# First modulation quarters as columns straight from the matrix engine, in a one-core hybrid encoder block

## The chip, the cores and the metric

The kernel runs on one core of a Trainium2 chip. The metric is the device time of one execution in microseconds (us). Engines are called PE (matrix engine), PEld (its weight loads), DVE (VectorE), ACT (ScalarE), POOL (GpSimd) and SP (the queue that issues most DMAs).

## The reference

One encoder layer on x of 1024 tokens by 1024 channels: a SwiGLU feed-forward, an attention mixer with two branches, and a second SwiGLU. Each of the three is modulated by shift, scale and gate vectors that come from one conditioning vector c. Only the start matters here:

```python
cond = jax.nn.silu(c)
mod = (cond @ ada_w[l] + ada_b[l]).reshape(B, N_SUBLAYERS, 3, D_MODEL)
h = modulate(x, norm_g[l, 0], mod[:, 0, 0], mod[:, 0, 1])      # rms_norm(x)*g*(1+scale)+shift
x = x + 0.5 * mod[:, 0, 2][:, None, :] * swiglu(h, ffn1_w1[l], ffn1_w3[l], ffn1_w2[l])
```

So no product of the first feed-forward can start before some channels of shift (`mod[:, 0, 0]`) and scale (`mod[:, 0, 1]`) are known: for each channel a sum of 1024 products of `cond` with a column of `ada_w`, a float32 matrix of 1024 by 9216.

## The kernel before, in words

x lies transposed in SBUF, channels on partitions: eight blocks of 128 channels, each in two halves of 512 tokens. The feed-forward's products run in "fp32 with reduced precision", split into a high and a low part (`wh`, `wl` for weights, `h` for the activations; three PE instructions for one product), with a Strassen-like scheme over pairs of column blocks (`UpPair`). They write the PSUM tiles named `y` and `b`.

A block c of h is made from x by DVE (`x <- x*A*rb`, with A the scale times the norm's gain and rb the norm's inverse root spread over partitions), by ACT (`h <- x + shift`, rounded) and by DVE again (the low part). `Operands.block` does that. So block c waits for A and shift of its 128 channels, which must stand as a column, one channel on a partition.

The first 512 channels of shift and scale are made in quarters of 256 channels, by `ModQuarter`. Quarter 0 serves blocks 0 and 1, quarter 1 blocks 2 and 3. Each quarter of each vector loads four tiles `mraw` of 256 KB, each with two chunks kc of 128 rows of `ada_w` by 256 columns. Blocks 4 to 7 are served by `ModHalf` (tiles `mraw` of 128x512, sums `macc` on DVE). In the kernel before there are two ways:

- `add` (for scale): DVE multiplies each chunk by its column of `cond` and adds it into `macc` (8 instructions of 128x256). Two float32 matmuls with `ones_col` then sum over partitions and give two columns.
- `row` (for shift): PE takes a column of `cond` as the stationary operand and streams the chunk past it (8 float32 matmuls with 256 columns, one row out). ACT copies the row to `mrow`, and two small matmuls turn it into columns.

`mod_done` adds the bias `ada_b` and, for scale, forms A with a second small DVE instruction. The root of the norm (`nacc`, `nv`, `na`, `nr`, then the matmuls with `ident`) is needed beside.

The code is recorded, not issued: `Plan` collects the instructions of a phase and places them engine by engine, in an order that it works out from due times and from its own costs of each instruction (`Plan.length`). All of the first feed-forward and the modulation is one such phase. Each engine then runs its instructions strictly in the order that was placed. While `nc.inorder` is set, SP's transfers keep the order of the code: x, quarter 0, four weight tiles `wr`, quarter 1, four more `wr`, and then the tiles of the halves.

Of the kernel before, what the change touches and what calls it, by code (L numbers as in the profile page):

```python
# [17 lines left out]
AF = mybir.ActivationFunctionType  # L18
ALU = mybir.AluOpType
# [38 lines left out]
class View:  # L58


    def __init__(self, tile, ops):
        self.tile, self.ops = tile, ops
# [115 lines left out]
class Plan:  # L178
# [29 lines left out]
    def take(self, engine, op, a, kw, calls=None, took=0.0):  # L208
        if not self.on:
            return self.issue(engine, op, a, kw)  # L210
        t = Task(len(self.tasks), engine, op, a, kw)
        t.rank, t.fixed = t.i + self.behind, self.inorder and engine == "sync"
        t.calls, t.took = calls or ((op, a, kw),), took
        self.tasks.append(t)
        writes, reads = [], []
        for _, b, w in t.calls:
            writes += [v for v in (b[0], w.get("accum_out")) if isinstance(v, View)]
            reads += [v for v in list(b[1:]) + [x for n, x in w.items() if n != "accum_out"] if isinstance(v, View)]
        before = set()
        for views, write in ((reads, False), (writes, True)):  # L220
            for v in views:
                r = v.region()
                for r2, j, w2 in v.tile.log:
                    if (write or w2) and j != t.i and all(p < q2 and p2 < q for (p, q), (p2, q2) in zip(r, r2)):
                        before.add(j)
        for views, write in ((reads, False), (writes, True)):
            for v in views:
                if write and not v.ops:
                    v.tile.log = []
                v.tile.log.append((v.region(), t.i, write))  # L230
        t.ready = max([getattr(v.tile, "written", 0.0) for v in reads] + [0.0])
        tiles = {id(v.tile): v.tile for v in reads + writes + self.wanted}
        self.wanted = []
        for x in tiles.values():
            if x.t is None and x.first is None:
                t.new.append(x)
                x.first = t.i
            elif x.t is None:
                before.add(x.first)
            x.uses += 1  # L240
        t.stored = op == "dma_start" and isinstance(a[0], View) and a[0].tile.pool.space == DRAM
        t.tiles = list(tiles.values())
        t.written = [v.tile for v in writes]
        for j in before:
            self.tasks[j].after.append(t)
        t.waits = len({self.tasks[j].engine for j in before} - {engine})
        t.left = len(before)
        out = writes[0] if writes else a[0]
        shape = list(out.shape)
        t.n, t.rows = int(np.prod(shape[1:])), shape[0]  # L250
        if op == "tensor_reduce":
            t.n = int(np.prod(a[1].shape[1:]))
        t.bytes = 4 * int(np.prod(shape))
        wide = [v for v in reads if int(np.prod(v.shape[1:])) > 8]
        sb = [v for v in wide if v.tile.pool.space != PSUM]
        if engine == "gpsimd":
            t.port = bool(sb) and op != "dma_start"
        elif engine == "vector":
            if op in ("tensor_scalar", "tensor_copy", "reciprocal"):
                t.port = len(sb) == 1 and "accum_out" not in kw and writes[0].tile.pool.space != PSUM  # L260
            else:
                t.port = len(sb) >= 2
        else:
            t.port = False
        if engine == "tensor" and not took:
            m = a[2] if op == "matmul" else a[1]
            t.exact = m.tile.dt in (F32R, BF16) or any(o[0] == "bitcast" and F32R in o[1] for o in m.ops)
# [22 lines left out]
    def length(self, t, e):  # L290

        n = t.n
        if t.op == "dma_start":
            return (0.35 if e == "sync" else 0.54), 0.0
        if e == "tensor":
            if t.took:
                return t.took, 0.23
            if t.exact:
                d = max(0.04, 0.003 + n / 2286.0)
            elif t.op == "transpose":  # L300
                d = n / 1174.0
            else:
                d = max(0.224, 0.009 + n / (595.0 if t.rows > 1 else 1200.0))
            return d, 0.23
        more = "accum_out" in t.kw
        if e == "scalar":
            ap = sum(isinstance(t.kw.get(x), View) for x in ("bias", "scale"))
            start = 0.07 if isinstance(t.a[1], View) and t.a[1].tile.pool.space == PSUM else 0.11
            return start + n / 1200.0 + (0.14 if more else 0.0) + (0.06 if ap else 0.0), 0.16
        if e == "gpsimd":  # L310
            if t.op in ("tensor_scalar", "memset"):
                return 0.24 + n / 1190.0, 0.105
            return 0.06 + n / 440.0, 0.105
        if t.op == "tensor_tensor_scan":
            d = 0.15 + n / 480.0
        elif t.op == "tensor_tensor_reduce":
            d = 0.075 + n / 960.0
        elif t.op == "scalar_tensor_tensor" or more:
            d = 0.13 + n / 960.0
        elif t.op == "tensor_scalar" and t.port:  # L320
            d = 0.075 + n / 1920.0
        else:
            d = 0.07 + n / 960.0
        return max(0.2, d), 0.145
# [238 lines left out]
class SquareSum:  # L563
# [5 lines left out]
    def add(self, x):  # L569
        nc = self.k.nc  # L570
        sq = t512(self.k, name="nsq" if self.acc else "nacc")
        nc.scalar.activation(sq, x, AF.Square)
        if self.acc:
            self.eng.tensor_add(self.acc, self.acc, sq)
        else:
            self.acc = sq
        return sq
# [150 lines left out]
def t512(k, dt=F32, name="t", home="c"):  # L728

    p, tag, n = k.homes[home]  # L730
    return p.tile([128, H], dt, tag=tag, name=name, bufs=n)
# [748 lines left out]
class ModHalf:  # L1480
# [24 lines left out]
    def columns(self):  # L1505

        t = self.bank()
        for b in range(4):
            self.k.nc.tensor.matmul(t[:, b:b + 1], self.acc[:, b * 128:b * 128 + 128], self.k.ones_col, start=True, stop=True)
        mod_done(self.k, self.i, t, 4 * self.h, 4)  # L1510
# [27 lines left out]
class ModQuarter:  # L1538
# [1 line left out]

    N = 256

    def __init__(self, k, i, q, bank):
        self.k, self.i, self.q, self.bank, self.raws = k, i, q, bank, []

    def load(self, g):
        k, n = self.k, self.N
# [3 lines left out]
                            k.ada_w[g * 256:g * 256 + 256, c0:c0 + n].rearrange("(a p) n -> p a n", p=128))  # L1551
        self.raws += [t[:, 0:n], t[:, n:2 * n]]

    def add(self):
        k, nc = self.k, self.k.nc
        acc = t512(k, name="macc")[:, 0:self.N]
        for kc, t in enumerate(self.raws):
            c = k.cond[:, kc:kc + 1]
            if kc == 0:
                nc.vector.tensor_scalar(acc, t, c, None, op0=ALU.mult)  # L1560
            else:
                nc.vector.scalar_tensor_tensor(acc, t, c, acc, op0=ALU.mult, op1=ALU.add)
        self.done(acc, k.ones_col)

    def row(self):
        k, nc = self.k, self.k.nc
        t = self.bank()[0:1, 0:self.N]
        for kc, r in enumerate(self.raws):
            nc.tensor.matmul(t, k.cond[:, kc:kc + 1], r, start=kc == 0, stop=kc == 7)
        r = t512(k, name="mrow")[0:1, 0:self.N]  # L1570
        nc.scalar.activation(r, t, AF.Copy)
        self.done(r, k.ones_col[0:1, :])

    def done(self, v, one):
        t = self.bank()
        for b in range(2):
            self.k.nc.tensor.matmul(t[:, b:b + 1], v[:, b * 128:b * 128 + 128], one, start=True, stop=True)
        mod_done(self.k, self.i, t, 2 * self.q, 2)


def side_by_side(gens):
# [641 lines left out]
def layer(tc, xT, c, pos, ada_w, ada_b, ng, inv, w13a, w2a, w_a, w_f, w_q, w_g, fb, fg, dg, wbr, wout, w13b, w2b, out):  # L2223
    with ExitStack() as es:
        k = K()
# [63 lines left out]
        with ExitStack() as ph:  # L2289
# [21 lines left out]
                q.first = True  # L2311
            ops = Operands(k, 0, x, nc.vector)
            mod = {i: ModHalf(k, i, 1, bank) for i in range(2)}
            quarter = [[ModQuarter(k, i, q, bank) for i in range(2)] for q in range(2)]
            k.up_step, k.stores = 0, []

            def consts():
# [54 lines left out]
            for i in range(8):  # L2372
                t = sq.add(x[i][0])
                if i < 4:
                    nc.tensor.matmul(warm, z.bitcast(F32)[:, 0:128], x[i][0], start=True, stop=True)
            for n in range(4):
                for m in quarter[0]:
                    m.load(n)
            for i in range(2):
                pairs[i].load1("c", (0,))  # L2380
            for n in range(4):
                for m in quarter[1]:
                    m.load(n)
            for i in range(2, 4):
                pairs[i].load1("c", (0,))
            nc.inorder = False
            rms[0] = norm_rms(k, sq.acc, rp, bank)
            ops.rb[0] = norm_spread(k, rms[0], bank)
            for m in quarter:
                m[1].add()  # L2390
                m[0].row()
            for c in range(4):
                ops.block(c)
            for i in range(4):
# [323 lines left out]
```

## Time and profile before

| | us |
|---|---|
| runs | 2113.15, 2115.29, 2115.32 |
| median of these | 2115.29 |
| the profiled execution | 2112.17 |
| its span in the trace | 2110.5 |
| PE busy of the span | 2094.6 |

The span is what the trace shows of the profiled execution, 1.7 us less than its own time. [...] A row of the timeline merges equal records that follow each other and gives start, time from the first start to the last end, and their number; the bracket says how long the engine was idle before and what ended that. Where a row says mean ns, that is the length of one record, and records of PE overlap.

### The profile page before, as it was taken

The numbers are of one execution on the slowest core, as the hardware profiler recorded it, in microseconds if no ns is written. First come the engines' busy times: TensorE is split into PE (matmuls) and PEld (weight loads), VectorE is DVE, ScalarE is ACT, GpSimd is POOL, SyncE is SP. The second block draws the span as 40 slices with busy tenths as digits, with TensorE's granted clock in tenths as the row PEclk, the third lists the DMA queues.
The fourth block names the chain that finished last, engine by engine and source line by source line (L and its number), as shares of the span: only waits on it lengthen the run. The fifth ranks groups of instructions, "written<-read, shape, count | busy, mean of one in ns | idle before, by whom it ended". The sixth has DMA issues, their size and how long they took to land.

```text
span 2110.5 us, 30999 instructions
## 1 busy us (share of the span) xinstructions
PE 2094.6 (99%) x10296; PEld 1728.2 (82%) x10296; DVE 1641.7 (78%) x3167; ACT 1135.6 (54%) x2075; POOL 251.1 (12%) x397
## 2 busy tenths in 40 slices
PE   8999999999999999999999999999999999999999
PEld 5887888888888888888888888888888888888887
DVE  7989887869977399886998877979975765568554
ACT  5754444445456266688776776335543333334443
POOL 0022222321100000000444332000000000000000
PEclk9999999999999999999999999999999999999999
DMA  9468888899721555668543224794142523375511
GB/s 347 134 215 275 303 295 274 277 379 366 261 92 48 172 174 192 217 244 274 192 158 99 86 66 160 252 315 154 46 130 100 194 85 129 101 264 206 189 50 41
DMA packets 218285, 398.72 MB, mean 189 GB/s; under 512 B 27198, under 2 KB 69694, under 8 KB 217100
## 3 DMA queue, kind: packets, MB, share of 16 engines
q1 hardware_dynamic: 199772, 339.24, 48.0%
q0 software_dynamic: 18064, 57.46, 7.1%
q8 instruction: 81, 1.33, 0.3%
q14 instruction: 80, 0.66, 0.1%
q10 hardware_dynamic: 288, 0.05, 0.0%
HBM read 282.62 MB, written 114.03 MB: 188 GB/s over the span
## 4 chain that ended last, share of the span: by engine, by line
PE 91%; issue 3%; DVE 2%; DMA 2%; ACT 1%; POOL 1%; SPq 0%; POOLq 0%; DVEq 0%; ACTq 0%
PE b L198 37%; PE y L198 28%; PE pj L198 12%; PE py L198 7%; PE p L198 4%; PE pt L198 4%; DMA mraw<-in_ada_w 0%; POOL d_g L198 0%; DMA f<-d_f 0%; DMA wr<-in_w13b 0%; ACT nt L198 0%; DMA d_wf10l<-pre 0%; DVE z L198 0%; DMA x<-in_xT 0%; ACT h L198 0%
## 5 line engine op out<-in xcount | busy, mean ns | idle before, releaser
L198 PE MATMUL b<-h,wh 128*128 128x512 f32 x1408 | 436.5, 390 | 0.5 <-DVE z L198 0.4
L198 PE MATMUL y<-h,wh 128*128 128x512 f32 x1280 | 397.1, 390 | 0.4 <-ACT h L198 0.3
L198 ACT ACTIVATE wh<-wr 128x512 fp32r<-128x512 f32 x308 | 192.6, 629 | 316.0 <-PE b L198 166.1
L198 PEld LDWEIGHTS b<-h,wh 128*128 128x128 f32 x1408 | 263.2, 188 | 59.1 <-DVE z L198 3.4
L198 PEld LDWEIGHTS y<-h,wh 128*128 128x128 f32 x1280 | 239.6, 188 | 53.4 <-issue 1.2
L198 DVE TENSOR_TENSOR wl<-wr,wh 128x512 fp32r<-128x512 f32 x308 | 208.4, 686 | 94.4 <-ACT wh L198 88.8
L198 PE MATMUL b<-h,wl 128*128 128x512 f32 x704 | 273.6, 389 | 0.0
L198 PE MATMUL y<-h,wl 128*128 128x512 f32 x640 | 249.0, 389 | 0.0
L198 PE MATMUL pj<-wh,h 128*128 128x512 f32 x512 | 161.3, 391 | 0.0
L198 PEld LDWEIGHTS b<-h,wl 128*128 128x128 f32 x704 | 132.2, 188 | 27.7
L198 PEld LDWEIGHTS y<-h,wl 128*128 128x128 f32 x640 | 120.1, 188 | 24.8
L198 ACT ACTIVATE wh<-g 128x512 fp32r<-128x512 f32 x154 | 96.0, 624 | 80.2 <-PE b L198 55.7
L198 PE MATMUL b<-wh 128*128 128x512 f32 x352 | 137.0, 389 | 0.7 <-ACT mrow L198 0.7
L198 DVE TENSOR_TENSOR wl<-a,wh 128x512 fp32r<-128x512 f32 x132 | 90.8, 688 | 59.9 <-ACT wh L198 55.7
L198 PE MATMUL b<-wl,wh 128*128 128x512 f32 x352 | 136.9, 389 | 0.0
L198 PE MATMUL b<-wh,wl 128*128 128x512 f32 x352 | 136.8, 389 | 0.0
L198 ACT ACTIVATE wh<-a 128x512 fp32r<-128x512 f32 x132 | 82.4, 625 | 99.9 <-PE b L198 60.3
L198 DVE TENSOR_TENSOR wl<-g,wh 128x512 fp32r<-128x512 f32 x154 | 105.6, 686 | 29.6 <-ACT wh L198 29.1
L198 POOL TENSOR_SCALAR pr<-pr,mn 128x128 f32<-128x128 f32 (+7 forms) x128 | 102.3, 816 | 167.3 <-DVE mn L198 135.1
L198 ACT ACTIVATE pth<-pt 128x512 fp32r<-128x512 f32 (+1 forms) x160 | 85.5, 554 | 55.9 <-PE pt L198 54.3
L198 DVE TENSOR_TENSOR ptl<-pt,pth 128x512 fp32r<-128x512 f32 (+1 forms) x160 | 97.9, 632 | 20.1 <-ACT pth L198 18.6
L198 PEld LDWEIGHTS pj<-wh,h 128*128 128x128 f32 x512 | 95.7, 188 | 18.6
(382 smaller groups left out, 4376.4 us busy)
## 6 DMA issues: line engine op xcount, KB each, us to landing
g<-d_g SPq DMA_DIRECT2D x154, 256.0 KB, 5.3
mraw<-in_ada_w SPq DMA_DIRECT2D x144, 256.0 KB, 5.7
wr<-in_w13a SPq DMA_DIRECT2D x112, 256.0 KB, 5.4
wr<-in_w13b SPq DMA_DIRECT2D x88, 256.0 KB, 4.8
d_g<-z POOLq DMA_DIRECT2D x77, 256.0 KB, 5.8
d_g<-z SPq DMA_DIRECT2D x77, 256.0 KB, 3.2
a<-in_w2a SPq DMA_DIRECT2D x44, 256.0 KB, 6.3
a<-in_w2b SPq DMA_DIRECT2D x44, 256.0 KB, 5.3
```

Of the source, the lines that this page charges most:

```text
L198: getattr(getattr(self.tc.nc, engine), op)(*map(real, a), **{n: real(v) for n, v in kw.items()})
```

## The change

Both ways of making a quarter are replaced by one, `columns`: the chunk itself (128x128 of it) is the stationary operand and the column of `cond` the moving one, so that a matmul gives one column of 128 channels; eight of them add up in PSUM. That is 16 float32 matmuls with one moving column for a quarter of one vector, 64 in all. The two columns of a quarter lie in two PSUM banks, and `mod_done` is called for each of them alone. DVE's sums, the rows, ACT's copies and the small matmuls behind them are gone. The loads of a quarter come in another order: the four tiles of shift, then the four of scale, instead of taking turns.

```diff
@@ Plan.length, float32 matmuls
-                d = max(0.224, 0.009 + n / (595.0 if t.rows > 1 else 1200.0))
+                d = max(0.112, 0.005 + n / 1200.0)
@@ ModQuarter
-    def add(self):
...
-    def row(self):
...
-    def done(self, v, one):
-        t = self.bank()
+    def columns(self, *banks):
+
+        k = self.k
+        ts = [bank() for bank in banks]
         for b in range(2):
-            self.k.nc.tensor.matmul(t[:, b:b + 1], v[:, b * 128:b * 128 + 128], one, start=True, stop=True)
-        mod_done(self.k, self.i, t, 2 * self.q, 2)
+            t = ts[b % len(ts)]
+            for kc, r in enumerate(self.raws):
+                k.nc.tensor.matmul(t[:, b:b + 1], r[:, b * 128:b * 128 + 128], k.cond[:, kc:kc + 1], start=kc == 0, stop=kc == 7)
+        for b in range(len(ts)):
+            mod_done(k, self.i, ts[b][:, b:], 2 * self.q + b, 2 // len(ts))
@@ layer
-            for n in range(4):
-                for m in quarter[0]:
+            for m in quarter[0]:
+                for n in range(4):
                     m.load(n)
...
-            for m in quarter:
-                m[1].add()
-                m[0].row()
+            for q in quarter:
+                for m in q:
+                    m.columns(bank, bank)
```

The planner's cost of every float32 matmul changes too (from at least 0.224 to at least 0.112 us), so the order of the whole phase is worked out anew.

On PE, from the first `mraw` to the first products, the rows before were these (`1x256` is the row way, the `ident` row spreads the norm's root):

```order
L198 MATMUL b<-mraw,cond 1x256 x2
L198 MATMUL b<-ones_col,nacc 128x1 x4
L198 MATMUL b<-mraw,cond 1x256 x6
L198 MATMUL b<-ones_col,mrow 128x1 x2
L198 MATMUL b<-ident,nr 128x128 x4
L198 MATMUL b<-ones_col,macc 128x1 x2
L198 MATMUL b<-mraw,cond 1x256 x2
L198 MATMUL y<-h,wh 128x512 x2
```

On PE at the same place the rows now are these:

```order
L198 MATMUL b<-cond,mraw 128x1 x4
L198 MATMUL b<-ones_col,nacc 128x1 x4
L198 MATMUL b<-cond,mraw 128x1 x19
L198 MATMUL b<-ident,nr 128x128 x4
L198 MATMUL b<-cond,mraw 128x1 x9
L198 MATMUL y<-h,wh 128x512 x3
```

All 32 matmuls of quarter 0 stand ahead of the first product, 28 of them behind the norm's sum. None of quarter 1 does; before, two of its eight did.

On PE behind the first products, where quarter 1 is made between them, the rows before were these:

```order
L198 MATMUL b<-mraw,cond 1x256 x2
L198 MATMUL y<-h,wh 128x512
L198 MATMUL y<-h,wl 128x512
L198 MATMUL y<-h,wh 128x512
L198 MATMUL b<-ones_col,mrow 128x1 x2
L198 MATMUL y<-h,wl 128x512
L198 MATMUL y<-h,wh 128x512
L198 MATMUL b<-ones_col,macc 128x1 x2
```

On PE the same stretch now begins like this:

```order
L198 MATMUL y<-h,wh 128x512 x3
L198 MATMUL b<-cond,mraw 128x1 x4
L198 MATMUL y<-h,wh 128x512
L198 MATMUL y<-h,wl 128x512
L198 MATMUL b<-cond,mraw 128x1 x4
L198 MATMUL y<-h,wh 128x512
L198 MATMUL b<-cond,mraw 128x1 x4
L198 MATMUL y<-h,wh 128x512
L198 MATMUL y<-h,wl 128x512
L198 MATMUL b<-cond,mraw 128x1 x4
L198 MATMUL y<-h,wh 128x512
```

Quarter 1 now comes in eight groups of four, each between one to three products. Before it came in three groups of two behind the first product, one pair for the row and one pair for `macc`. Behind the last of the eight groups stand eleven products on blocks 0 and 1, then the first one on block 2.

On DVE the fourteen `macc<-mraw,cond,macc` of 128x256 and the two that begin them are gone. Its first `x<-x,A,b` stands behind all four small `mod` additions of quarter 0 and the A of block 0, and the first wide `macc` (128x512) stands behind the h of block 3, as it did before.

On ACT, at the end of the operands of the first feed-forward (`h<-x,mod` of its last blocks), the rows before were these:

```order
L198 ACTIVATE wh<-wr 128x512 x2
L198 ACTIVATE h<-x,mod 128x512
L198 ACTIVATE z<-y 128x512 x2
L198 ACTIVATE z<-z 128x512
L198 ACTIVATE wh<-wr 128x512
```

On ACT they now are these:

```order
L198 ACTIVATE wh<-wr 128x512
L198 ACTIVATE h<-x,mod 128x512 x2
L198 ACTIVATE z<-y 128x512
L198 ACTIVATE wh<-wr 128x512
L198 ACTIVATE z<-y 128x512
```

One more `h<-x,mod` stands ahead of the copy `z<-y` that empties a PSUM bank, and one `wh<-wr` between the two copies.

More of the change, by code (lines that the diff above doesn't have):

```diff
@@ L249, in take @@
         shape = list(out.shape)
-        t.n, t.rows = int(np.prod(shape[1:])), shape[0]
+        t.n = int(np.prod(shape[1:]))
         if op == "tensor_reduce":
@@ L1541, with __init__ @@
     N = 256
-    def __init__(self, k, i, q, bank):
-        self.k, self.i, self.q, self.bank, self.raws = k, i, q, bank, []
+    def __init__(self, k, i, q):
+        self.k, self.i, self.q, self.raws = k, i, q, []
     def load(self, g):
@@ L1552, in load @@
         self.raws += [t[:, 0:n], t[:, n:2 * n]]
-    def add(self):
[L1555 to L1563, printed above, removed]
-    def row(self):
[L1566 to L1572, printed above, removed]
-    def done(self, v, one):
-        t = self.bank()
-        for b in range(2):
-            self.k.nc.tensor.matmul(t[:, b:b + 1], v[:, b * 128:b * 128 + 128], one, start=True, stop=True)
-        mod_done(self.k, self.i, t, 2 * self.q, 2)
+    def columns(self, *banks):
+        k = self.k
+        ts = [bank() for bank in banks]
+        for b in range(2):
+            t = ts[b % len(ts)]
[3 more added lines that the diff above has]
+            mod_done(k, self.i, ts[b][:, b:], 2 * self.q + b, 2 // len(ts))
 def side_by_side(gens):
@@ L2313, in layer @@
             mod = {i: ModHalf(k, i, 1, bank) for i in range(2)}
-            quarter = [[ModQuarter(k, i, q, bank) for i in range(2)] for q in range(2)]
+            quarter = [[ModQuarter(k, i, q) for i in range(2)] for q in range(2)]
             k.up_step, k.stores = 0, []
@@ L2380, in layer @@
                 pairs[i].load1("c", (0,))
-            for n in range(4):
-                for m in quarter[1]:
+            for m in quarter[1]:
+                for n in range(4):
                     m.load(n)
```

## The prediction

> **What bounds the kernel.** First the page's busy times, then a table by stages.
>
> ```profile
> PE 2094.6 (99%) x10296; PEld 1728.2 (82%) x10296; DVE 1641.7 (78%) x3167; ACT 1135.6 (54%) x2075; POOL 251.1 (12%) x397
> ```
>
> ```profile
> 10.00:20.00 10.00, 7.35 (x42) 4.12 (x43) 9.00 (x29) 3.48 (x6) 0.00 (x0) 1.00 1.09 364
> 20.00:30.00 10.00, 9.73 (x42) 5.16 (x41) 7.75 (x18) 2.80 (x5) 0.00 (x0) 1.00 1.08 371
> 1600.00:1800.00 200.00, 200.00 (x883) 164.66 (x882) 125.46 (x197) 75.78 (x130) 0.00 (x0) 1.00 0.38 128
> ```
>
> The columns are PE, PEld, DVE, ACT and POOL busy, the granted clock, the DMA share and GB/s. PE is the bound: it has work in all but 16 us of the span of 2110.5, and from 20 us on hardly pauses, at the full clock. So a microsecond of PE work added behind the first product is a microsecond of span, and so is a delay of the first product. The change lies wholly in 10 to 35 us. There the timeline of PE is read.
>
> ```profile
> 10.95 1.02 PE L198 MATMUL b<-mraw,cond 128*1 128x256 f32 x4 [1.16 <-DMA mraw<-in_ada_w]
> 12.05 1.05 PE L198 MATMUL b<-ones_col,nacc 128*128 128x1 f32 x8
> 13.03 1.89 PE L198 MATMUL b<-mraw,cond 128*1 128x256 f32 x8
> 15.39 1.02 PE L198 MATMUL b<-mraw,cond 128*1 128x256 f32 x4 [0.47 <-DMA mraw<-in_ada_w]
> 16.88 0.60 PE L198 MATMUL b<-ones_col,mrow 1*128 1x1 f32 x4 [0.46 <-ACT mrow L198]
> 17.41 1.16 PE L198 MATMUL b<-ident,nr 128*128 128x128 f32 x8
> 18.41 0.50 PE L198 MATMUL b<-ones_col,macc 128*128 128x1 f32 x4
> 19.60 1.02 PE L198 MATMUL b<-mraw,cond 128*1 128x256 f32 x4 [0.69 <-DMA mraw<-in_ada_w]
> 20.89 0.73 PE L198 MATMUL y<-h,wh 128*128 128x512 f32 x2 [0.27 <-ACT h L198]
> ...
> 25.62 0.40 PE L198 MATMUL y<-h,wl 128*128 128x512 f32 x1
> 25.86 0.39 PE L198 MATMUL y<-h,wh 128*128 128x512 f32 x1
> 26.17 1.02 PE L198 MATMUL b<-mraw,cond 128*1 128x256 f32 x4
> 27.12 0.50 PE L198 MATMUL y<-h,wh 128*128 128x512 f32 x1
> 27.46 0.40 PE L198 MATMUL y<-h,wl 128*128 128x512 f32 x1
> 27.70 0.39 PE L198 MATMUL y<-h,wh 128*128 128x512 f32 x1
> 28.02 0.60 PE L198 MATMUL b<-ones_col,mrow 1*128 1x1 f32 x4
> 28.55 0.50 PE L198 MATMUL y<-h,wl 128*128 128x512 f32 x1
> 28.88 0.40 PE L198 MATMUL y<-h,wh 128*128 128x512 f32 x1
> 29.12 0.50 PE L198 MATMUL b<-ones_col,macc 128*128 128x1 f32 x4
> 29.48 0.49 PE L198 MATMUL y<-h,wh 128*128 128x512 f32 x1
> ```
>
> The first product comes at 20.89, released by ACT's h. From there PE takes what its queue holds, one after the other.
>
> **The price of a matmul, from grouped rows** (busy in all, then mean ns of one record):
>
> ```profile
> L198 PE MATMUL b<-mraw,cond 128*1 128x256 f32 x32 | 8.0, 378 | 2.3 <-DMA mraw<-in_ada_w 2.3
> L198 PE MATMUL b<-ones_col,mrow 1*128 1x1 f32 x8 | 1.2, 250 | 0.5 <-ACT mrow L198 0.5
> L198 PE MATMUL b<-ones_col,nacc 128*128 128x1 f32 x8 | 1.1, 253 | 0.1
> L198 DVE SCALAR_TENSOR_TENSOR macc<-mraw,cond,macc 128x256 f32<-128x256 f32 x14 | 6.7, 482 | 0.2
> L198 DVE TENSOR_SCALAR macc<-mraw,cond 128x256 f32<-128x256 f32 x2 | 0.7, 346 | 0.0
> ```
>
> The new matmul (128x128 stationary, one column moving, float32) is the form of `ones_col,nacc`: four of them are eight records, which start (1.05 - 0.25)/7 = 0.114 us apart, so 0.23 a matmul. The row way streams 256 columns past one: (1.02 - 0.38)/3 = 0.214 a record, 0.43 a matmul. The `mrow` records start (0.60 - 0.25)/3 = 0.117 apart. All of PE's share before: 32 x 0.214 + 8 x 0.117 + 8 x 0.114 (`macc`) = 8.7 us. Now: 64 x 2 x 0.114 = 14.6. So **PE gets 5.9 us more**, and DVE is rid of 6.7 + 0.7 = 7.4. The question is how much of the 5.9 falls into PE's pauses before 20.89.
>
> [...]
>
> **Term 1, the first product.** Two rows of DVE first, the last step of the norm's root and the last sums of scale:
>
> ```profile
> 16.41 0.15 DVE L198 SCALAR_TENSOR_TENSOR nr<-na,nr 128x4 f32<-128x4 f32 x1
> 16.53 1.01 DVE L198 SCALAR_TENSOR_TENSOR macc<-mraw,cond,macc 128x256 f32<-128x256 f32 x2
> ```
>
> So the root was there by 16.6 and the last tile of quarter 0 by about 17.0, when the second of these sums began. Walk the new order with these numbers. The first four matmuls start with the first tile, at 10.95 as before, and take 8 x 0.114 = 0.9. The norm's sum stays at 12.05, since it waits for DVE's `nacc`; the next work starts at 13.03. Then 19 matmuls: 38 x 0.114 = 4.3, to 17.36. The `ident` group takes 17.41 to 18.41 = 1.0, to 18.36; its input, the root, is there. Nine more matmuls: the last record starts 17 x 0.114 later, at 20.30, and ends at 20.55. PE reaches the last tile's chunks after 18.36, so it waits for no transfer. Before, the last `macc` record ended at 18.41 + 0.50 = 18.91, and this chain followed:
>
> ```profile
> 18.95 0.17 DVE mod L198
> ...
> 19.14 0.17 DVE A L198
> ...
> 19.34 0.76 DVE x L198
> ```
>
> From that end to the first product: 1.98. Now A of block 0 is done one column earlier, and x follows the fourth `mod` directly, so the step of 0.20 from `mod` to A drops out: 1.78. First product at 20.55 + 1.78 = 22.3, **1.4 later**. Bounds: if the new small operations, one column wide (the trace has two columns, 0.16 us), or the gaps come out otherwise, 0.5 to 2.0.
>
> **Term 2, quarter 1 between the products.** A group costs its records, the change of form, and slower products beside it. Around 26.17: the product before starts 0.31 ahead of the group (two products in a row: 0.23 to 0.24), the next product 0.95 behind the group's start (four records are 0.86), and that one takes 0.34 until its successor. So a group costs 0.29 besides its records. Before, behind the first product: three groups of 0.86 + 0.29, the `mrow` pair (28.55 - 27.70 less 0.23, and 0.10 behind it: 0.72) and the `macc` pair (29.48 - 28.88 less 0.23, and 0.10 again: 0.47) = 4.6. Now eight groups of 8 x 0.114 + 0.29 = 1.20: 9.6. **5.0 later.** Bounds 3.5 to 5.5, as the switch costs 0.1 or 0.3. Its DMAs land in time: PE comes to them later than before. The chain to block 2 (1.98 from its last sum) has eleven products as cover, 11 x 0.227 (200 us by 883 in the last stage quoted) = 2.5; if the cover fails, its 2.0 in part. What is lost here finds no pause of PE later in which it could be made up.
>
> **Term 3, DVE's late start.** DVE's relief is worth nothing by itself: its next wide work, the halves' sums, stands behind the h of block 3 in both orders, so it idles where `macc` was and starts these sums as late as PE comes. Then it has no slack:
>
> ```profile
> 32.80:110.90 78.10, 75.51 (x133) 1.00 0.56 190
> ```
>
> ```profile
> 109.49 0.73 ACT L198 ACTIVATE h<-x,mod 128x512 fp32r<-128x512 f32 x1 [0.40 <-DVE h L198]
> 110.88 1.26 ACT L198 ACTIVATE z<-y 128x512 f32<-128x512 f32 x2 [0.66 <-DVE h L198]
> ```
>
> ```profile
> 111.53 0.73 PE L198 MATMUL y<-h,wh 128*128 128x512 f32 x2 [0.17 <-ACT z L198]
> ```
>
> DVE is busy 75.5 of 78.1 us; ACT's `z<-y` waits for DVE, and PE for ACT's copy. The new order has one more `h<-x,mod` (0.73) ahead of this copy, and it waits for DVE too. So PE waits longer: **1.0 more**, nearest to that 0.73 with a part of DVE's step; bounds 0 (the wait stays as it is) and 2.6 (all of DVE's idle time in the stretch).
>
> The rest of the first phase gets another order of the same instructions. PE's waits there, from 140 to 640 us, were these two:
>
> ```profile
> PE b L198 <- ACT mrow L198: 0.7, 1, 0.7
> PE b L198 <- DVE z L198: 0.4, 1, 0.4
> ```
>
> Nothing else can be won, and I take 0, with bounds of 1.1 less (both gone) and 1.5 more (as many again, and a little).
>
> **The sum.** 1.4 + 5.0 + 1.0 = 7.4. On the profiled execution, 2112.17: 2119.6. The median of the runs is 3.1 above that execution, which gives 2122.7; the four times known average 2114.0, which gives 2121.4. I take 2121.4.
>
> **The rivals.**
>
> - *Half the price.* The changed planner has 0.112 us for such a matmul, one record's worth. If that were so (7.3 us in all), the `ident` group would start with the root at 16.6 and end at 17.6, the nine behind it at 18.6, and the first product come 0.5 earlier; the eight groups would cost 8 x (0.46 + 0.29) = 6.0, 1.4 more than before, and term 3 would go: 2114.0 + 0.9 = 2114.9, no change. Against it stands the row of `nacc`. Chance 0.11.
> - *Covered.* PE's work as priced, but the pauses ahead of 20.89 (1.16, 0.47, 0.46, 0.69, 0.27) and freed DVE time take most of it: only 1.5 to 3.5 left, 2116.5. Against it: the order puts all of quarter 1 behind the first product. Chance 0.09.
> - *Hidden loads, faster.* If the weight loads of so short matmuls hid behind each other and the records started a quarter as far apart (0.03), quarter 0 would end with its last tile at 17.0, the first product would come at 17.3 + 0.25 + 1.78 = 19.3, 1.6 earlier; the eight groups would cost 8 x (0.24 + 0.29) = 4.2, 0.4 less; and an early DVE would spare PE the wait on `z<-y` (0.4 with the slower product behind) and up to 1.1 later: 3.5 less in all, 2110.5. It turns faster where a matmul costs less than about 0.1. Against it: eight `nacc` records have the same loads and keep 0.114. Chance 0.03.
> [...]
>
> **How the numbers follow.** Forecast, slower by 3 to 11.6: 0.74. All lower bounds together (0.5 + 3.5 + 0 - 1.1 = 2.9) give 2116.9, all upper ones (2.0 + 5.5 + 2.6 + 1.5 = 11.6) 2125.6; with a part of "covered" the range is 2116 to 2126. A measurement of this kernel tells about 0.2%, 4.2 us, from no change. Faster by more, half of "hidden loads" and a little: 0.02. Within: half price, covered, the rest: 0.22. Slower by more: 0.76, the forecast nearly whole and "four passes".
>
> **What would show it.** Right: a first product at about 22.3; `b<-cond,mraw` with 128 records 0.11 apart, four to a group between products until about 33 us; DVE idle for some microseconds between 10 and 20 us; a wait of PE on `z<-y` of over 1 us near 117. Wrong: 64 records instead of 128; the first product at or before 20.9; a wide `macc` before 33 us; products of the second hundred less than 4 us later than before.

## The result, and the profile after

| | before | after |
|---|---|---|
| median of 4 runs each, us | 2114.22 | 2137.73 |
| lowest to highest | 2112.47 to 2115.32 | 2137.39 to 2139.44 |
| the profiled execution | 2112.17 | 2137.84 |
| its span | 2110.5 | 2136.1 |

The ratio is 1.0114, with a 95% interval of 1.0096 to 1.0131; the medians differ by 23.5 us, so the change makes the kernel slower. The sign was forecast; the size was not, and lies outside the range.

The page of the changed kernel, busy times first, then the granted clock in 40 slices of the span:

```profile
PE 2115.4 (99%) x10376; PEld 1755.3 (82%) x10376; DVE 1633.9 (76%) x3157; ACT 1134.4 (53%) x2073; POOL 250.5 (12%) x397
PEclk6999999999999999999999999999999999999999
```

PE has 20.8 us more than before, where the sum of the prediction had given it 5.9. The first slice of the clock shows a 6. The table by stages of the changed kernel (columns as before: PE, PEld, DVE, ACT, POOL, clock, DMA share, GB/s) splits that slice:

```profile
10.00:20.00 10.00, 8.73 (x54) 8.68 (x54) 4.31 (x17) 2.12 (x4) 0.00 (x0) 0.72 1.09 364
20.00:30.00 10.00, 8.30 (x37) 7.93 (x37) 4.36 (x10) 3.20 (x6) 0.00 (x0) 0.50 1.08 371
30.00:40.00 10.00, 10.00 (x43) 9.42 (x42) 1.67 (x5) 0.22 (x1) 0.00 (x0) 0.50 1.04 384
40.00:60.00 20.00, 20.00 (x76) 17.09 (x77) 10.66 (x20) 6.70 (x12) 0.00 (x0) 0.70 0.58 192
60.00:100.00 40.00, 40.00 (x194) 33.63 (x193) 35.98 (x69) 26.19 (x47) 1.33 (x2) 1.00 0.47 141
```

Before, the clock was 1.00 in each of these stages. Now it is **half from about 14.4 us** (0.72 over ten us is 5.6 us at 0.5) **to about 52 us** (0.70 over twenty is 12 us at 0.5): 37.5 us. It fell while PE was at work, at 8.73 of 10 us busy. PE's timeline of the changed kernel shows it from inside:

```profile
11.19 1.02 PE L198 MATMUL b<-cond,mraw 128*128 128x1 f32 x8 [1.37 <-DMA mraw<-in_ada_w]
12.29 1.05 PE L198 MATMUL b<-ones_col,nacc 128*128 128x1 f32 x8
13.21 7.13 PE L198 MATMUL b<-cond,mraw 128*128 128x1 f32 x38
20.20 2.05 PE L198 MATMUL b<-ident,nr 128*128 128x128 f32 x8
22.04 3.84 PE L198 MATMUL b<-cond,mraw 128*128 128x1 f32 x18
27.58 1.65 PE L198 MATMUL y<-h,wh 128*128 128x512 f32 x3 [1.70 <-ACT h L198]
29.02 1.70 PE L198 MATMUL b<-cond,mraw 128*128 128x1 f32 x8
30.58 0.77 PE L198 MATMUL y<-h,wh 128*128 128x512 f32 x1
...
46.80 0.77 PE L198 MATMUL y<-h,wh 128*128 128x512 f32 x1
```

The first eight new records take 1.02, as `nacc` did; eight of them at 29.02 take 1.70, and the `ident` group 2.05 where it took 1.16. All of PE runs at about half speed, products included (two in a row 0.43 us apart, 0.23 before), until quarter 1 is done at 46.80 and for five microseconds more. The 128 records themselves, two for each of the 64 matmuls, in the grouped rows of the changed kernel:

```profile
L198 PE MATMUL b<-cond,mraw 128*128 128x1 f32 x128 | 25.6, 327 | 1.4 <-DMA mraw<-in_ada_w 1.4
```

Two further lines of the changed kernel, DVE's timeline and PE's wait on the copy:

```profile
25.07 0.16 DVE L198 TENSOR_TENSOR mod<-b,ada_b 128x1 f32<-128x1 f32 x1 [7.52 <-PE b L198]
```

```profile
134.34 0.73 PE L198 MATMUL y<-h,wh 128*128 128x512 f32 x2 [2.27 <-ACT z L198]
```

DVE stands idle for 7.52 us in the head, waiting for PE's columns, and PE waits 2.27 on `z<-y` where it waited 0.17.

Where the delay arises is read from the starts of four records in each trace (the first, 51st and 201st `y<-h,wh`, and the first `y<-wh` of the next stage), here with the kernels of the experiments:

| start, us | before | after | e1 | e8 | e6 | e7 | e10 | e11 |
|---|---|---|---|---|---|---|---|---|
| first product | 20.9 | 27.6 | 22.5 | 20.8 | 22.0 | 27.1 | 33.4 | 21.1 |
| 51st | 68.2 | 88.9 | 72.3 | 71.3 | 70.9 | 76.6 | 76.0 | 67.1 |
| 201st | 136.2 | 159.0 | 142.4 | 141.4 | 140.3 | 145.4 | 143.3 | 135.2 |
| first `y<-wh` | 514.2 | 538.4 | 521.3 | 520.8 | 518.3 | 522.2 | 520.2 | 514.5 |

In the changed kernel 20.7 us of delay are there at the 51st product, 2.1 come by the 201st, 1.4 by 538 us. The rest of the span adds 1.4.

### The profile page after: what moved, and what is told of

Read it like the earlier page. It is cut to its first block, busy times and chain, and to the rows that moved or that the text cites. A ratio compares the mean times of both kernels' runs of the same rounds, so it can differ in the third digit from the quotient of the medians.

```text
span 2136.1 us, 31177 instructions
## 1 busy us (share of the span) xinstructions
PE 2115.4 (99%) x10376; PEld 1755.3 (82%) x10376; DVE 1633.9 (76%) x3157; ACT 1134.4 (53%) x2073; POOL 250.5 (12%) x397
## 4 chain that ended last, share of the span: by engine, by line
PE 87%; issue 5%; DMA 3%; DVE 2%; POOL 1%; ACT 1%; SPq 0%; POOLq 0%; DVEq 0%; ACTq 0%
PE b L198 34%; PE y L198 27%; PE pj L198 12%; PE py L198 7%; PE p L198 4%; PE pt L198 4%; DMA wr<-in_w13a 1%; POOL d_g L198 1%; DMA wr<-in_w13b 0%; DVE nacc L198 0%; DMA nat<-d_qkv 0%; ACT nt L198 0%; DMA d_wg3l<-pre 0%; DMA d_wg5l<-pre 0%; DVE h L198 0%
```

## The experiments

The theory is that the halved clock makes most of the loss, and that the one moving column of the new matmuls is what halves it. Against it stand the price of the new matmuls on any clock, and the new order.

**e1_wide128.** The order of every engine stays; each new matmul streams 128 equal columns instead of one:

```diff
-  k.nc.tensor.matmul(t[:, b:b + 1], r[:, b * 128:b * 128 + 128], k.cond[:, kc:kc + 1], ...)
+  k.nc.tensor.matmul(t[:, 0:128], r[:, b * 128:b * 128 + 128], k.cond[:, kc:kc + 1].to_broadcast([128, 128]), ...)
```

> The changed kernel with one thing different: the moving operand of the 64 column matmuls is the column of cond read 128 times (a broadcast), so 128 equal columns come out instead of one. Order of instructions on every engine, weight loads, loads and sums stay as they are. Theory A (the granted clock: with one moving column the array does next to nothing, the clock is halved from 14.5 to 52 us, and about 16 of the 23.5 us are this): the clock stays 1.00 throughout, the records start 0.11 apart all through, the first product comes at 22 to 22.6 us instead of 27.6, and the time is 2114.2 + 7.4 = about 2121.6 (2119 to 2124). Theory B (the 23.5 us come from PE's work and the new order, the clock is only a by-product): time within 3 us of 2137.7. Theory C (a matmul with 128 moving columns costs more than its weight load): clock 1.00 but records 0.15 or more apart, first product after 24 us, 2126 or more.

Measured: 2122.97 (2121.04 to 2123.18), ratio 1.0042 (1.0025 to 1.0059), as theory A has it. So **a matmul with 128 times as many columns is 14.8 us faster for the kernel**. The stages of this kernel, then its PE timeline:

```profile
10.00:20.00 10.00, 9.91 (x78) 8.69 (x77) 4.38 (x18) 2.20 (x4) 0.00 (x0) 1.00 1.09 365
20.00:30.00 10.00, 8.30 (x63) 7.56 (x63) 6.03 (x14) 3.64 (x6) 0.00 (x0) 1.00 1.07 373
40.00:60.00 20.00, 20.00 (x98) 16.82 (x97) 17.86 (x31) 14.25 (x28) 0.00 (x0) 1.00 0.97 320
```

```profile
13.38 4.49 PE L198 MATMUL b<-cond,mraw 128*128 128x128 f32 x38
17.70 1.05 PE L198 MATMUL b<-ident,nr 128*128 128x128 f32 x8
18.60 2.17 PE L198 MATMUL b<-cond,mraw 128*128 128x128 f32 x18
22.46 1.02 PE L198 MATMUL y<-h,wh 128*128 128x512 f32 x3 [1.70 <-ACT h L198]
...
24.45 0.39 PE L198 MATMUL y<-h,wl 128*128 128x512 f32 x1
24.67 1.05 PE L198 MATMUL b<-cond,mraw 128*128 128x128 f32 x8
25.48 0.48 PE L198 MATMUL y<-h,wh 128*128 128x512 f32 x1
25.80 1.05 PE L198 MATMUL b<-cond,mraw 128*128 128x128 f32 x8
```

The clock stays at 1.00 throughout the head. (It falls once, for 3.4 us, at 1464.7 us, far behind the change.) All four executions show the same: the mean clock of their spans is 0.999 to 1.000, against 0.989 to 0.992 in the changed kernel. The longest pause is that of the changed kernel (1.70 before the first product in both), and there the clock held, so the pause is not what made it fall. Beside that, this run gives the price at the full clock: eight records, then the next product 0.81 after the group's start (25.48 - 24.67), and that product takes 0.32 to its successor. With the 0.23 of two products in a row a group costs 0.81 + 0.32 - 0.23 = 0.90.

**e2_wide32 and e5_wide64.** The same edit with 32 and with 64 columns, one run each.

> As e1, with 32 moving columns. It asks how much streaming the clock asks for. Theory A with a threshold below a quarter of the time streaming: clock 1.00, same time as e1. A with a higher threshold: the clock falls as in the changed kernel, 2135 to 2139. Theory B: 2137 in either case.

> As e1_wide128, but with 64 moving columns. The order of every engine is again that of the changed kernel. 32 columns left the clock to fall, 128 held it. If the clock goes by the share of time in which columns stream (128 columns fill most of a record's 0.10 us, 32 about a quarter, 64 about a half), this run tells on which side a half lies: held, it gives e1_wide128's time, 2120 to 2125; fallen for some 37 us from about 14 us, 2136 to 2143, as the changed kernel. No forecast between the two.

Measured: 2141.91, above the 2135 to 2139 expected for a clock that falls, and 2129.52. First a stage of the kernel with 32 columns, then stages of that with 64:

```profile
10.00:20.00 10.00, 9.77 (x53) 8.96 (x52) 4.26 (x17) 2.23 (x4) 0.00 (x0) 0.68 1.09 364
```

```profile
15.00:20.00 5.00, 5.00 (x46) 4.96 (x45) 0.78 (x6) 1.26 (x2) 0.00 (x0) 1.00 1.08 369
20.00:22.00 2.00, 0.31 (x2) 0.22 (x2) 1.87 (x6) 0.99 (x2) 0.00 (x0) 1.00 1.11 352
22.00:24.00 2.00, 2.00 (x13) 1.64 (x13) 2.00 (x4) 1.39 (x3) 0.00 (x0) 0.89 1.09 355
24.00:28.00 4.00, 4.00 (x19) 3.81 (x18) 1.56 (x3) 1.26 (x2) 0.00 (x0) 0.50 1.05 383
```

With 32 columns the clock fell as with one, at 9.77 of 10 us busy, to 0.50 from about 13.6 us on. With 64 it held through the dense block of records to 20 us, and fell at 23.6, behind PE's pause at 20 to 22 us, for 20.5 us. That was neither of the two outcomes expected: in this one run 64 columns held the clock where PE was dense, and not with a pause beside. With the like pause (1.69 here, 1.70 there) e1's 128 columns had held it. The shares of a record's time named beforehand are an estimate from the row way, where 256 columns take 0.214: 32, 64 and 128 would take 0.027, 0.054 and 0.107, beside e1's records 0.10 apart. That the clock goes by this share was not shown.

**e3_rows and e4_q1_columns.** e3 makes all four vectors as rows (no sums on DVE), e4 makes quarter 0 as before and quarter 1 as columns of one. Both, and e6 below, have the planner's cost line and the load order of the change, so a part of their time belongs to the plan (see e7). The edits in outline; in e3 the old `row` stands in `ModQuarter` again:

```diff
 e3:  for q in quarter:
          for m in q:
-             m.columns(bank, bank)
+             m.row()
 e4:  quarter[0][1].add(); quarter[0][0].row()
      for m in quarter[1]:
          m.columns(bank, bank)
```

> All four vectors of the quarters made by the old row way (one column of cond stationary, 256 columns streamed), none on DVE: PE's work is 64 records of 0.214 and 16 small ones, 15.6 us, even more than the 14.6 of the columns, with the order worked out anew. Theory A: clock 1.00, and only the added PE work and its delays: 2119 to 2125. Theory B (PE's work and DVE's late start make the 23.5 us): 2133 or more, since as much work is added in the same place.

> Quarter 0 made as before the change (sums on DVE and a row), quarter 1 as columns with one moving column, four between one to three products. Asks whether columns between products alone lower the clock. Theory A: if products are 25 to 45% of PE's time there, the clock may hold; then 2117 to 2121 (5.0 of term 2). If it falls: first product near 21, products at 0.43 apart for some 10 to 30 us, 2125 to 2137. Theory B: 2117 to 2125 without a change of clock.

Measured, one run each: 2127.00, above the 2119 to 2125 expected since the clock fell here too, and 2127.29, inside the range for a clock that falls. The stages in which the clock fell, first of e3, then of e4:

```profile
18.00:22.00 4.00, 3.54 (x22) 1.86 (x21) 0.00 (x0) 0.81 (x3) 0.00 (x0) 1.00 1.10 350
22.00:26.00 4.00, 2.02 (x6) 0.75 (x7) 3.68 (x8) 2.97 (x6) 0.00 (x0) 0.69 1.08 369
30.00:40.00 10.00, 10.00 (x41) 3.76 (x40) 0.16 (x1) 1.37 (x4) 0.00 (x0) 0.98 1.06 388
```

```profile
14.00:18.00 4.00, 2.25 (x12) 1.00 (x10) 3.75 (x13) 1.57 (x3) 0.00 (x0) 1.00 1.07 373
18.00:22.00 4.00, 3.63 (x20) 3.67 (x20) 2.78 (x9) 1.66 (x4) 0.00 (x0) 0.63 1.10 349
30.00:40.00 10.00, 10.00 (x41) 9.32 (x40) 2.08 (x7) 0.72 (x1) 0.00 (x0) 0.50 1.05 385
```

In e3 rows kept the clock as long as PE was dense: one stationary column, 256 moving ones, 1.00 until 22 us with 3.54 to 4.00 us of work in each stage of four. Together with e1, where only the moving columns differ from the changed kernel, the clock of these runs went with the columns that move, not with the size of what is held. In both kernels a stage of four microseconds with PE half busy stands at the fall (e3: 2.02 of 4, with the fall at 23.5 within it; e4: 2.25, just ahead of the fall at 19.0); the last section shows that such a stage alone did not decide it. With rows and products the clock was back after 6.8 us (e3), while with columns of one it stood at 0.50 for 23.9 us (e4).

**e6_wide128_q1.** e4 with 128 columns.

> Quarter 0 made as before (shift as a row, scale by sums), quarter 1 as columns with 128 moving columns, so that the clock should hold. Tells term 1 from term 2. If e1's 4.1 us by 35 us are the sum of 1.6 for the first product and 2.5 for quarter 1 between the products, the first product comes within 0.6 us of before and block products from the 14th on are 2 to 3 us later. If the later waits (PE on ACT's z<-y) come from DVE's late start in quarter 1, they stay as in e1, at 2 to 2.5 us, and the time is 2118 to 2122; if they are a matter of the order that the planner finds, they differ, and the time is 2115 to 2118.

Measured: 2120.23 (10 runs, 2117.41 to 2121.25), ratio 1.0029 (1.0019 to 1.0038). The clock stayed at 1.00 in the profiled execution, which is the fastest of the ten (in the others its mean is 0.997 to 1.000, so in some of them it fell for a while). The time is in the range expected, but the parts are not: the first product came 1.1 later than before and the 51st 2.7, which leaves 1.6 for quarter 1; PE's wait on `z<-y` was 1.59.

**e7_planner_cost.** The kernel before, with one line of the change:

```diff
-                d = max(0.224, 0.009 + n / (595.0 if t.rows > 1 else 1200.0))
+                d = max(0.112, 0.005 + n / 1200.0)
```

> The kernel before with the planner's one changed cost line and nothing else: all instructions the same, in another order. Theory: the order by itself costs less than 2 us, 2112 to 2117, the first product within 1 us of before. Rival: the waits that appeared after 100 us in the changed kernel belong to the planner's new order, not to the columns: then PE's wait on z<-y is over 1.5 us here too and the time 2117 to 2121.

Measured: 2122.60 (2122.04 to 2123.33), ratio 1.0043 (1.0028 to 1.0058). Neither theory had this: **a line that computes nothing costs 8.8 us**, and 6.2 of them are there at the first product. The timeline of PE in this kernel, and its stages:

```profile
11.89 1.05 PE L198 MATMUL b<-ones_col,nacc 128*128 128x1 f32 x8 [2.17 <-DVE nacc L198]
16.85 2.05 PE L198 MATMUL b<-ident,nr 128*128 128x128 f32 x8 [3.91 <-DVE nr L198]
...
19.05 4.24 PE L198 MATMUL b<-mraw,cond 128*1 128x256 f32 x14
```

```profile
14.00:18.00 4.00, 1.15 (x5) 1.18 (x6) 3.79 (x14) 1.26 (x2) 0.00 (x0) 0.55 1.07 373
```

The plan puts `ident` ahead of the rows, PE waits 3.91 for the norm's root with work behind it that could run, and the clock falls to half in the pause (6.8 us from 14.4, and 3.4 us again from 28.0). The wait on `z<-y` is there too, with 1.08.

**e8_loads_interleaved.** e1 with shift's and scale's weights loaded by turns, as before the change (the two loops of `load` exchanged back).

> e1_wide128 with the weights loaded in the old order (shift and scale by turns) instead of shift first. Theory: the order of loads is worth nothing, since the columns of a quarter are all needed before its first block: first product within 0.4 us of e1's 22.46 and 2121 to 2125. Rival: shift first lets PE begin its records a transfer earlier, so that here the first product comes 0.5 to 1.5 us later and the time is 2124 to 2127.

Measured: 2123.50 (2121.87 to 2124.82), ratio 1.0045 (1.0029 to 1.0062): the same time as e1, by other steps than expected. The first product comes 1.7 *earlier* than e1's, as its row shows:

```profile
17.07 3.51 PE L198 MATMUL b<-cond,mraw 128*128 128x128 f32 x30
20.77 1.02 PE L198 MATMUL y<-h,wh 128*128 128x512 f32 x3 [0.20 <-ACT h L198]
```

Behind the last column PE waits 0.20 for h, where it waits 1.70 with shift first. In e1 scale's columns come last, and the steps from `mod` to h follow with nothing on PE beside them. At the 51st product 1.0 of the gain is left, at 520 us 0.5, in the medians nothing.

**e9_short_sums.** e1 with the halves' accumulating sums on 128 of 512 columns, all orders kept:

```diff
@@ ModHalf.add, the sums of blocks 4 to 7
+                out = self.acc[:, 0:512]
+                if self.h == 1 and self.i < 2:
+                    out.cut = 128
-                nc.vector.scalar_tensor_tensor(self.acc, self.raws[kc], c, self.acc, op0=ALU.mult, op1=ALU.add)
+                nc.vector.scalar_tensor_tensor(out, self.raws[kc], c, self.acc, op0=ALU.mult, op1=ALU.add)
@@ Plan.issue, after the planning
+        if getattr(a[0], "cut", 0):
+            a = [v[:, 0:a[0].cut] if list(v.shape)[-1] == 512 else v for v in a]
```

> e1_wide128 with all orders kept, but DVE's 14 accumulating sums of the two halves (macc, between 37 and 48 us) work on 128 of their 512 columns: the other columns of these sums are left out, so DVE has some 14 x 0.5 = 7 us less to do there. Theory: PE's wait on z<-y near 115 us is DVE's backlog, begun late because quarter 1 ends later on PE: the wait of 2.42 falls below 0.4, and the time to about 2120.5 to 2121.5. Rival: it is the order on ACT (h<-x,mod in front of z<-y) and its own chain: the wait stays above 2 and the time at 2122 to 2124.

Measured: 2123.34 (2120.15 to 2124.51). The sums in this kernel, DVE's timeline, and PE's wait:

```profile
L200 DVE SCALAR_TENSOR_TENSOR macc<-mraw,cond,macc 128x128 f32<-128x128 f32 x14 | 3.9, 344 | 0.1
```

```profile
82.57 0.69 DVE L200 TENSOR_TENSOR z<-y,z 128x512 f32<-128x512 f32 x1 [0.20 <-PE y L200]
88.01 0.69 DVE L200 TENSOR_TENSOR z<-y,z 128x512 f32<-128x512 f32 x1 [0.28 <-PE y L200]
```

```profile
117.53 0.73 PE L200 MATMUL y<-h,wh 128*128 128x512 f32 x2 [2.26 <-ACT z L200]
```

DVE was relieved of 5.6 us (these sums are 3.9 us of its time, and 9.5 in e1), and the wait did not move. DVE waits for PE at 82.57 and 88.01, so nothing of an earlier backlog is left there. **The theory fell.** The wait is still one for DVE: from 88.01 to 116.9 us DVE is busy for 28.75 of 28.89 us, and ACT's `z<-y` at 116.88 stood 0.60 us waiting for DVE's `wr`.

**e10_planner_cost_old.** e1 with the old cost line: the same instructions, planned anew.

> e1_wide128 with the planner's cost line of before (0.224 for such a matmul, which is what two records of 0.10 take). The plan is another: all 64 column matmuls stand in one block behind ident, ahead of the first product. Theory: PE's work is the same, only its place moves: first product at 30 to 33 us, 30 products later within 2 us of e1's, and 2121 to 2125 in all. Rival: the block waits for the root (nr) with PE idle before it, the clock falls in the pause as in e7_planner_cost, and the time is 2126 to 2132.

Measured: 2120.29 (5 runs, 2119.62 to 2121.95), ratio 1.0033 (1.0021 to 1.0045). PE's timeline of it, and one stage:

```profile
15.69 2.05 PE L198 MATMUL b<-ident,nr 128*128 128x128 f32 x8 [2.52 <-DVE nr L198]
17.53 16.10 PE L198 MATMUL b<-cond,mraw 128*128 128x128 f32 x128
33.38 0.71 PE L198 MATMUL y<-h,wh 128*128 128x512 f32 x2
```

```profile
22.00:26.00 4.00, 4.00 (x39) 4.00 (x38) 2.37 (x6) 0.10 (x1) 0.00 (x0) 1.00 1.08 368
```

The clock fell in the pause before `ident` (14.1, for 6.8 us), and stood at 1.00 again from 22 us on, in the dense records of 128 columns. The first product is 10.9 later than e1's and the 51st 3.7; from 105 to 130 us PE has no wait on ACT at all, and by the first `y<-wh` this kernel is 1.1 *ahead* of e1. Theory and rival both failed in part: the clock fell, but the time lies below either range, and after 30 products it was still some 3.6 behind e1, where 2 at most had been expected.

**e11_shift_wide and e12_shift_wide_first.** The kernel before with shift alone as columns of 128 as in e1, for which no copy by ACT is needed; e12 loads shift first besides.

```diff
             for m in quarter:
                 m[1].add()
-                m[0].row()
+                m[0].columns(bank, bank)
```

> The kernel before, with shift's row alone replaced by columns of 128 moving columns, scale by DVE's sums as before, old load order and old planner cost. PE's price by e1's records: 8 x 0.20 = 1.6 us a half quarter pair of columns (16 matmuls, 3.2) against 8 x 0.43 + 0.5 = 3.9 for the row, so 0.7 less in each quarter, and the pause of 0.46 for ACT's mrow is gone. Theory: first product 0.3 to 0.8 earlier than before and 2112 to 2114. Rival: the planner's new order adds waits of its own, as in e7, and the time is 2115 to 2119.

> e11_shift_wide with shift's weights loaded first. Its order has all of shift's columns of quarter 1 in one block ahead of the first product. Theory: the first product comes 1.5 to 3 us later than e11's and the products from the 30th on at the same time, 2112 to 2115 in all. Rival: as in e11.

Measured: 2114.59 (11 runs, 2112.94 to 2117.65), ratio 1.0004 (0.9995 to 1.0013), and 2114.50 (10 runs, 2113.39 to 2119.56), ratio 1.0006 (0.9997 to 1.0015). No difference from before can be told. e11's first product came 0.2 later than before, not 0.3 to 0.8 earlier. Its groups of eight records take 0.80 to the next product, so the price of the columns shows as expected, and 1.1 us are gained at the 51st product; but a wait for weights (1.65 before 20.19, with the first product queued behind it) keeps the first product from coming earlier, and by the first `y<-wh` the gain is spent:

```profile
20.19 1.13 PE L198 MATMUL b<-cond,mraw 128*128 128x128 f32 x8 [1.65 <-DMA mraw<-in_ada_w]
```

e12's first product comes 5.4 us after e11's, not the 1.5 to 3 expected: its block of 32 records, from 20.03 on, ran at half clock until 26.1. But this trace is of the slowest of its ten executions (2119.56); another, of 2114.57, had a mean clock of 1.000, so the fall is not in all of them. No kernel of the study beats the one before.

## Why the prediction was wrong

**The step that failed** is the assumption under all three terms: that PE works "at the full clock". Its rows showed 1.00 for the kernel before, and I carried that over to a kernel whose PE does something else from 11 to 46 us. The price of 0.114 us for a record was right at 11.19, where eight take 1.02; at 29.02 eight take 1.70. At half clock PE loses at most 37.5 x 0.5 = 18.8 us. Between the changed kernel and e1, whose edit changes nothing but the moving columns, the 51st product shows 88.9 - 72.3 = 16.6, the medians 14.8. No term, bound or rival held a clock that falls.

**Term 1**, 1.4 for the first product, was about right at the full clock: 22.46 in e1 against 20.89, 1.6 later, with the wait for h at 1.70. e8 adds what I did not see: with the loads by turns that wait is 0.20, so it is the order of the loads that leaves this chain bare.

**Term 2**, 5.0 for quarter 1, was twice too high even at the full clock. From e1 the 51st product is 4.1 late, less 1.6 leaves 2.5. The mis-sized piece is the 0.29 that was added to every group for the change of form. The records come as far apart as priced, (1.05 - 0.27)/7 = 0.11 with 0.27 for the length of one, but the 0.29 had been read beside the row way; in e1 a group costs 0.90 in place of 1.20, its eight records and nothing more. So 8 x 0.90 = 7.2 against 4.6 before. That is the price of 128 columns; what a group of one column costs at the full clock no run shows.

**Term 3**, 1.0 for the wait on `z<-y`, was too small, and the reason that gave it its name was wrong. PE's wait rose from 0.17 to 2.26 in e1. DVE's late start was to make it; e9 took most of that work away and the wait stayed. e7, with no column at all, has 1.08, so at least a part comes with the new plan. The size, though, had been taken from another row, the one more `h<-x,mod` ahead of the copy, and that row is there in ACT's timeline of e1:

```profile
115.84 0.72 ACT L198 ACTIVATE h<-x,mod 128x512 fp32r<-128x512 f32 x1 [0.40 <-DVE h L198]
117.17 0.60 ACT L198 ACTIVATE z<-y 128x512 f32<-128x512 f32 x1 [0.60 <-DVE wr L198]
```

From its wait for DVE to the copy it takes 1.7 us. Whether it alone makes the wait was not settled: no run moved it by itself. e10 has no such wait, but there DVE's wide sums begin earlier (30.8 for 37.1) and the 51st product comes 3.7 later, so it does not single out the order.

**The rest**, taken as 0: from the 201st product to the first `y<-wh` e1 loses 0.9 more, inside the bounds.

The sum of 7.4 lies close to e1's 8.9 (0.42% of 2114; the medians of that session differ by 10.0). That is luck and does not bear the terms out: one was too large, one too small. In the traces e1 is 7.1 late at the first `y<-wh` and 10.8 over the span. The last 3.7 come far behind the change, where the prediction had nothing; a wait of PE for `nacc` (1.32 before 1463.56, none in the kernel before) and the clock's fall at 1464.7 are among them.

**The rivals.** "Half the price" and "hidden loads" are out: 128 records came, 0.11 apart at the full clock. "Covered" is out too, since all of quarter 1 stood between products. The "four passes" that the chances count under slower by more are shown by no run: at the full clock the records stand 0.11 apart, as priced, and with the same weight loads and the same number of records the kernel takes 2122.97 in e1. (How often a float32 matmul passes through PE was not shown either: each of its two records takes 0.214 for 256 columns in the row way, where the one record of a product takes 0.227 for 512.) And a rival was missing that e7 shows: the planner's cost line alone was worth 8.8 us on the kernel before, 6.2 of them by PE's wait for the root and the clock that fell in it. The changed kernel's own plan has no such wait; the order that I had read told that, but I never priced what a plan can lose.

The signs named beforehand read so: 128 records came, as told, but 0.21 apart; DVE idled 7.52 us; the wait on `z<-y` was 2.27; the first wide `macc` came at 50.7. That spacing, the first product (27.58 for 22.3) and the end of quarter 1 (46.8 for about 33) are where the clock shows.

## What to carry to other kernels

The clock of 1.00 read from the kernel before did not carry over to the changed one, which had 0.50 for 37.5 us: where an edit fills tens of microseconds of PE with matmuls of few moving columns (1 and 32 here), price it at the full and at the half clock, with the products beside it. One edit that streams more columns at the same order tells in one run which of the two it is. Where a planner sets the order, test a change of its costs on the unchanged kernel by itself, since the plan alone can move the time as much as the work does.

## What the runs showed of the hardware that had not been expected

- With a stationary of 128x128 float32 and 1 or 32 moving columns the granted clock fell to 0.50 within stages with PE busy for 8.73 and 9.77 of 10 us; with 128 moving columns it stayed at 1.00 in the same order through the head (9.91 of 10 us busy in that stage), and with 64 it did while PE was dense (5.00 of 5 us), in one run.
- The clock also fell in kernels with rows (e7) and with 128 columns (e10 and e12): each has 6.8 us at 0.50, beside windows of four microseconds with 1.05, 2.37 and 2.24 us of PE work. The work in such a window did not decide it, though, since e11 kept the clock at 1.00 with 2.35. The row of e12, stage 14 to 18 us, with the fall at 19.2 behind it, and that of e11, stage 18 to 22 us, which held:

```profile
14.00:18.00 4.00, 2.24 (x21) 2.08 (x20) 3.72 (x16) 0.82 (x2) 0.00 (x0) 1.00 1.07 373
```

```profile
18.00:22.00 4.00, 2.35 (x19) 2.17 (x18) 3.89 (x9) 3.08 (x5) 0.00 (x0) 1.00 1.10 351
```

- The stretches at half clock in the heads are 3.4 (e7), 6.8 (e3, e7, e10, e12), 20.5 (e5), 23.9 (e4) and 37.5 us (the changed kernel) long. What sets their length no run tested, nor why the clock falls in one execution of a kernel and not in another (e12: a mean of 0.998 in that of 2119.56, 1.000 in that of 2114.57).
- 128 moving columns cost PE hardly more than one here: eight records take 1.05 us in e1 (at 24.67) and 1.02 with one column at the full clock (at 11.19 in the changed kernel).
